# Separate pools for meta-token and rotary tiles, a later load of the key latents, and squares through PSUM in an encoder block

## The chip, the cores and the metric

One Trainium2 chip, one core. The time is device microseconds of one execution. Of its engines, TensorE (PE) multiplies into PSUM, VectorE (DVE), ScalarE (ACT) and GpSimd (POOL) work elementwise, and SyncE (SP) only issues transfers, one after another. PSUM has eight banks of 128 x 512 fp32.

## The reference

The kernel computes one layer on 1024 tokens with 16 learned meta tokens ahead of them (L = 1040), width 1024, in fp32:

```python
u = rmsnorm(h, norm_mix_w)
rq, rk, rv, rg, a_cq, a_ckv, a_kr, a_gret, a_gmla = split(u @ w_in)
y_ret = (silu(rg) * head_group_norm(bidir_retention(rope(rq), rope(rk) / 8, rv))) @ w_ret_out
c_q, c_kv = rmsnorm(a_cq, q_norm_w), rmsnorm(a_ckv, kv_norm_w)        # ranks 384 and 256
q_nope, q_rope = split_heads(c_q @ w_uq);  q_rope = rope(q_rope);  k_rope = rope(a_kr)
k_nope, v = c_kv @ w_uk, c_kv @ w_uv
y_mla = attention(q_nope, q_rope, k_nope, k_rope, v) @ w_mla_out      # 8 heads
h = h + (sigmoid(a_gret) * y_ret + sigmoid(a_gmla) * y_mla) @ w_o
u = rmsnorm(h, norm_ffn_w)
h = h + (silu(u @ w_ffn_gate) * (u @ w_ffn_up)) @ w_ffn_down          # 2816 wide
out = rmsnorm(h, norm_final_w)[16:]
```

## The kernel before

All large products run in split precision: an operand becomes a high part (a cast on ACT) and a low part (a subtraction on DVE, `split`, L153 and L154, and L209 and L210 for weights), and three matmuls of 128 x 512 give one product. Most products use seven block products instead of eight (`seven` and `seven_out`): four 512-wide weight blocks are loaded, POOL forms their sums (L191 to L193, L207), `prod` runs the matmuls of one block product (L217), and `seven_out` combines the banks on DVE (L233 to L242) and hands four result blocks to a `post` function. The order of instructions on each engine is chosen ahead of the run by a list scheduler with its own model of time, which goes by the order of the program where several instructions are ready; each engine and the queue of SyncE then run in that order. A tile is taken from a pool with a fixed number of buffers; its next user waits until all users of the buffer are done, a transfer's landing included.

The stages that the change touches:

1. **Last projections** (about 540 to 600 us). After the retention core, `project_key` (projects the last third of the query latent and the shared key) and `project_kv` (the key-value latent) run. Each also has a tail for the 16 meta tokens: matmuls of 48 rows (L222) gather them in one PSUM bank, `meta_sum` adds two parts (L431 on ACT, L432 on DVE), a transposition (L779, L802) turns them, `latent_part` and `shared_key` scale, square, split and store them (L724 to L734, L750 to L764), and `latent_norm` makes the factors `sq_c` and `skv_c` (L160, L741 to L744). All of these tiles, even the 16-column ones, come from the pool `cr`, which has six buffers of 128 x 512 and serves the results of all projections too. `rest_gates` (L813) also takes a buffer of `cr` and loads a saved partial result `e_d` into it. Between these, `z_split` loads 28 tiles `z_d` of retention results (L839), four buffers deep, and splits them (L275, L276).
2. **Retention output pairs** (about 598 to 691 us). `ret_out(0)`, a second, a `third` and `ret_out(3)`, each 84 matmuls. Their block products go through four PSUM banks (`pm`), and `pc` has the other four. Their `ret_post` loads a gate tile from `g_d` into `cr` (L856), multiplies (L857) and stores `r_d` (L858). Meanwhile six query latents `cq` and four key latents `ckv` (high and low parts, two each), 512 and 520 KB each, are loaded (L909), spread over the pairs by `tc.issue_after`, and `skv_b`, a row broadcast to all partitions (L915). Matmuls on `cq` make the rotary queries; `rotary` (L890 to L900), called by `third_post` four times, takes two table tiles per half and two tiles per call from `cr`, turns them and stores `qr`.
3. **Start of attention** (from about 679 us). `heads_k` multiplies `ckv` (`t<-ckh,kh`), DVE scales by `skv_b` into `kf` (L973); `heads_q` multiplies `cq`; the values `vt` need `ckv` too (`o<-vh,ckh`).
4. **Output projection** (`w_o`, about 1016 to 1108 us). For each token half `c` and block `m`: 24 matmuls, a residual addition on DVE (L1216), scaled blocks and, for `c` = 1, the block sums for the seven-product scheme (L1226 to L1240, one subtraction on POOL at L1236), then the square on ACT (L1245) and its addition to `ssum[c]` on POOL (L1246). `norm(c)` sums over partitions with eight matmuls of one column (L1197), takes root and reciprocal (L1201, L1202) and spreads the result with matmuls (L174) and a copy (L177).
5. **Feed-forward gate.** The first pair's first four block products are begun for three of the four input blocks, before the rest.

Of the kernel before, what the change touches and what calls it, by code (L numbers as in the profile page):

```python
# [17 lines left out]
P = 128  # L18
# [3 lines left out]
NM = 16  # L22
# [26 lines left out]
def build(nc, tc, A, out):  # L49
# [133 lines left out]
    def seven(pools, srcs, blocks, meta=None):  # L183
# [10 lines left out]
        side = {"11": a11, "t2": s2, "t3": a21, "n1": s1, "21": a12, "t4": a22, "22": s2}  # L194
        banks, w, begun = {}, {}, []

        def prod(b, qs=range(nq)):
            k = BANK[b]
            begins = k not in banks
            if begins:  # L200
# [51 lines left out]
    with ExitStack() as c1:  # L252
# [69 lines left out]
        with ExitStack() as c2:  # L322
# [89 lines left out]
            with tc.issue_after(made[0].ins), tc.issue_after(made[1].ins):  # L412
# [3 lines left out]
                for q in range(4):  # L416
                    U[q]["22"] = bsplit("22", x22[q])
            rest_out([(seven(w7, win(0), U), es[0], rg_post(0)),
                      (seven((wb, wf, wh1, wl1, pc), win(1), U), es[1], rg_post(1))], cr)
        mf = sb(mid, "factor", 1, side="right")  # L420
        rstd_b = mk(mf, (P, L), "rstd_b")
        lss = mk(mf, (P, L), "lss")
# [6 lines left out]
        def meta_sum(ps, lo, n):  # L429
            t = slot(cr)[:NM, :n]  # L430
            act.copy(t, ps[32:48, lo : lo + n])  # L431
            dve.tensor_add(t, ps[0:NM, lo : lo + n], t)  # L432
            return t
# [115 lines left out]
        def project_rope(j, key):  # L549
# [19 lines left out]
            if key:  # L569
                x = meta_sum(ps, 0, 256).rearrange("t (h c) -> t h c", c=64)  # L570
                y = slot(cr)[:NM, :256].rearrange("t (h c) -> t h c", c=64)

# [148 lines left out]
        def latent_part(t, c, dst, col, first):  # L721
            n = c.stop - c.start
            hi = slot(cr, F32R)[:, :n]
            act.mul(hi, t, col)  # L724
            if first:
                act.square(lss[:, c], t)
            else:
                q = slot(cr)[:, :n]
                act.square(q, t)
                dve.tensor_add(lss[:, c], lss[:, c], q)  # L730
            lo = slot(cr)[:, :n]
            dve.scalar_tensor_tensor(lo, t, col, f(hi), ALU.mult, ALU.subtract)
            store(dst[0][:, c], f(hi))
            store(dst[1][:, c], lo)  # L734
# [14 lines left out]
        def shared_key(ks, c):  # L749
            n = c.stop - c.start  # L750
            ca, sa = slot(cr)[:48, :n], slot(cr)[:48, :n]
            load(ca, A["cM"][:48, c])
            load(sa, A["sM"][:48, c])
            sb_, kh = slot(cr)[:48, :n], slot(cr, F32R)[:48, :n]
            dve.tensor_mul(ks, ks, rstd_b[:48, c])
# [34 lines left out]
        def project_key():  # L790
# [11 lines left out]
            pe.transpose(pt[:48, :NM], t, ident[:NM, :NM])  # L802
            ks = slot(cr)[:48, :NM]
            act.copy(ks, pt[:48, :NM])
# [60 lines left out]
        cq = [(mk(ap, (P, S), f"cqh{k}", F32R), mk(ap, (P, S), f"cql{k}", F32R)) for k in range(3)]  # L865
        ckv = [tuple(mk(ap, (P, 1152), f"ck{j}{k}", F32R)[:, :L] for j in "hl") for k in range(2)]
        swp = sb(right, "skv", 1, side="right")
        skv_b = mk(swp, (P, L), "skv_b")
        fill(swp, 112)
        wa = sb(right, "wa", 1, side="right")  # L870
        rot = ExitStack()
        wt = sb(rot, "rotary", 1, side="right")

        qr_d = [[mk(dram, (P, S), f"qr{i}{j}") for j in range(2)] for i in range(2)]
        wx, xx, tables = [], {}, []

        def wx_load(i):
            raw = slot(cr)[:, :384]
            load(raw, A["w_uq"][4 + i])
            hi = mk(wa, (P, 384), ("qh", "qr")[i], F32R)  # L880
            low = mk(wt, (P, 384), "xl", F32R) if i else mk(wa, (P, 384), "ql", F32R)
            act.copy(hi, raw)
            dve.tensor_sub(low, raw, f(hi))
            wx.append((hi, low))

        def rotary(lo, n, i):
            c = slice(lo, lo + n)
            if i == 0:
                tables[:] = slot(cr), slot(cr)
                load(tables[0], A["cM"][:, c])  # L890
                load(tables[1], A["sM"][:, c])
            ta, tb_ = slot(cr), slot(cr)
            dve.tensor_mul(ta, xx[lo, i], tables[0])
# [11 lines left out]
        wx_load(1)  # L905
        for i, (dst, src) in enumerate([(t, cq_d[k][j]) for k in range(3) for j, t in enumerate(cq[k])] + [
                (t, ckv_d[k][j]) for k in range(2) for j, t in enumerate(ckv[k])]):
            with tc.issue_after(issued[1 + i * 3 // 5].ins):
                load(f(dst), src)  # L909
# [4 lines left out]
        store(n_d, rowc)  # L914
        load(skv_b, n_d.rearrange("b i -> (b i)")[:L].unsqueeze(0).broadcast_to([P, L]))  # L915
        third = seven(w7, A["w_ro"][2], Z)
# [11 lines left out]
        seven_out(third, cr, third_post)  # L928
        rot.close()
        ret_out(3)  # L930

# [204 lines left out]
    with ExitStack() as c1:  # L1136
# [71 lines left out]
        for c in range(2):  # L1208
            for m in range(KT):
# [21 lines left out]
                else:  # L1231
# [3 lines left out]
                    t7["t2"] = split(t2, bt, bt)  # L1235
                    pool.tensor_sub(g12, g12, g22)  # L1236
                    t7["t3"] = split(g12, bt, bt)
# [3 lines left out]
                if m == 0:  # L1241
                    act.square(ssum[c], hm)
                else:
                    t = slot(xr)
                    act.square(t, hm)  # L1245
                    pool.tensor_add(ssum[c], ssum[c], t)  # L1246
            norm(c, slice(0, 512))

        w7 = (wr3, ws3, wh3, wl3, pm)
        for j in range(11):  # L1250
# [19 lines left out]
            if j == 0:  # L1270
                for b in NAMES[:4]:
                    prod(b, range(3))
                    rest[b] = range(3, 4)
            seven_out(prod, xr, gate_post, rest)
# [182 lines left out]
```

## Time and profile before

| | us |
|---|---|
| median of 3 timed runs | 1775.89 (1775.68 to 1776.03) |
| the profiled execution | 1780.81 |
| its span, first to last instruction | 1779.0 |
| TensorE busy in the span | 1714.6 |
| granted clock, mean over the span | 0.987 of full speed |

The time of a run is about that of the profiled span; the profiled execution was 4.9 us slower than the median of the timed runs. TensorE's busy time counts matmuls that overlap in a pipeline, so a stretch at full pace shows about 112 matmuls of 512 columns in 25 us.

### The profile page before, as it was taken

The numbers are of one execution on the slowest core, as the hardware profiler recorded it, in microseconds if no ns is written. First come the engines' busy times: TensorE is split into PE (matmuls) and PEld (weight loads), VectorE is DVE, ScalarE is ACT, GpSimd is POOL, SyncE is SP. The second block draws the span as 40 slices with busy tenths as digits, with TensorE's granted clock in tenths as the row PEclk, the third lists the DMA queues.
The fourth block names the chain that finished last, engine by engine and source line by source line (L and its number), as shares of the span: only waits on it lengthen the run. The fifth ranks groups of instructions, "written<-read, shape, count | busy, mean of one in ns | idle before, by whom it ended". The sixth has DMA issues, their size and how long they took to land.

```text
span 1779.0 us, 26433 instructions
## 1 busy us (share of the span) xinstructions
PE 1714.6 (96%) x8804; PEld 1443.9 (81%) x8804; DVE 1339.0 (75%) x2448; ACT 861.1 (48%) x1614; POOL 790.1 (44%) x605
## 2 busy tenths in 40 slices
PE   8999999999999899999999999899999999999997
PEld 6788777788887677899998888788888888787787
DVE  7845778788888857888888758767666666987965
ACT  7425766344324523788787346433332232543434
POOL 1322257674554321234332524666676566533422
PEclk9999999999999899999999999999999999999999
DMA  7733823566546785111112754233323333854512
GB/s 255 240 101 119 295 85 117 180 201 213 189 158 230 213 301 179 28 34 40 30 59 69 231 187 162 66 101 119 101 95 101 107 105 101 286 176 123 154 57 95
DMA packets 145433, 253.59 MB, mean 143 GB/s; under 512 B 18889, under 2 KB 36738, under 8 KB 145298
## 3 DMA queue, kind: packets, MB, share of 16 engines
q1 hardware_dynamic: 145298, 251.92, 43.5%
q8 instruction: 69, 1.13, 0.3%
q14 instruction: 66, 0.54, 0.1%
HBM read 174.93 MB, written 76.85 MB: 142 GB/s over the span
## 4 chain that ended last, share of the span: by engine, by line
PE 49%; DVE 7%; DMA 3%; ACT 3%; issue 2%; SPq 0%; POOL 0%; DVEq 0%; ACTq 0%; POOLq 0%
PE mm L217 29%; PE o L1041 3%; PE mm L138 3%; PE mm L137 3%; PE mm L139 3%; PE t L1012 2%; DVE slot L154 2%; PE s L137 1%; PE s L138 1%; PE s L139 1%; DMA slot<-g_d 1%; DMA slot<-f_d 1%; DVE slot L210 1%; DVE ptl L1015 1%; PE o L137 1%
## 5 line engine op out<-in xcount | busy, mean ns | idle before, releaser
L217 PE MATMUL mm<-slot,slot 128*128 128x512 f32 x2604 | 598.3, 392 | 8.4 <-ACT slot L209 3.7
L217 PEld LDWEIGHTS mm<-slot,slot 128*128 128x128 f32 x2604 | 490.6, 189 | 115.0 <-DVE slot L210 5.5
L209 ACT CAST slot<-slot 128x512 fp32r<-128x512 f32 (+1 forms) x413 | 246.1, 598 | 465.9 <-PE mm L217 395.0
L210 DVE TENSOR_TENSOR slot<-slot,slot 128x512 fp32r<-128x512 f32 (+1 forms) x413 | 361.6, 877 | 71.5 <-ACT slot L209 70.4
L217 PE MATMUL mm<-ht,slot 128*128 128x512 f32 x648 | 219.6, 400 | 7.4 <-DVE slot L210 3.4
L217 PE MATMUL mm<-h,slot 128*128 128x512 f32 x536 | 184.4, 403 | 0.0
L191 POOL TENSOR_TENSOR slot<-slot,slot 128x512 f32<-128x512 f32 (+1 forms) x61 | 85.3, 1398 | 220.0 <-DMA slot<-in_w_u 50.7
L207 POOL TENSOR_TENSOR slot<-slot,slot 128x512 f32<-128x512 f32 (+1 forms) x61 | 84.7, 1390 | 185.1 <-DVE slot L210 173.1
L217 PEld LDWEIGHTS mm<-ht,slot 128*128 128x128 f32 x648 | 122.1, 190 | 35.1 <-DVE slot L210 5.6
L154 DVE TENSOR_TENSOR slot<-slot,slot 128x512 fp32r<-128x512 f32 x137 | 117.5, 872 | 20.6 <-ACT slot L153 20.0
L217 PE MATMUL mm<-lt,slot 128*128 128x512 f32 x324 | 128.7, 397 | 0.0
L153 ACT CAST slot<-slot 128x512 fp32r<-128x512 f32 x137 | 83.3, 619 | 76.9 <-DMA slot<-f_d 30.3
L192 POOL TENSOR_TENSOR slot<-slot,slot 128x512 f32<-128x512 f32 (+1 forms) x61 | 86.0, 1410 | 77.6 <-DVE slot L210 65.6
L217 PEld LDWEIGHTS mm<-h,slot 128*128 128x128 f32 x536 | 101.2, 190 | 21.6 <-DVE slot L210 0.6
L1002 DVE TENSOR_SCALAR_CACHE_REDUCE pr<-s,sq_c 128x384 f32<-128x384 f32 (+1 forms) x192 | 103.3, 573 | 7.9 <-PE t L1020 3.8
L217 PE MATMUL mm<-l,slot 128*128 128x512 f32 x268 | 106.6, 398 | 0.0
L139 PE MATMUL mm<-slot,slot 128*128 128x512 f32 (+1 forms) x288 | 105.3, 366 | 0.0
L138 PE MATMUL mm<-slot,slot 128*128 128x512 f32 (+1 forms) x288 | 105.3, 366 | 0.0
L137 PE MATMUL mm<-slot,slot 128*128 128x512 f32 (+1 forms) x288 | 105.1, 367 | 0.0
L1015 DVE TENSOR_TENSOR ptl<-t,pth 128x512 fp32r<-128x512 f32 x128 | 85.7, 685 | 18.2 <-ACT pth L1014 17.6
L1046 POOL TENSOR_TENSOR oa<-oa,ob 64x256 f32<-64x256 f32 x32 | 24.0, 751 | 154.5 <-ACT ob L1045 149.1
L193 POOL TENSOR_TENSOR slot<-slot,slot 128x512 f32<-128x512 f32 (+1 forms) x61 | 88.2, 1445 | 1.4
(365 smaller groups left out, 3506.0 us busy)
## 6 DMA issues: line engine op xcount, KB each, us to landing
slot<-in_w_in SPq DMA_DIRECT2D x106, 256.0 KB
f_d<-slot SPq DMA_DIRECT2D x71, 256.0 KB
slot<-f_d SPq DMA_DIRECT2D x71, 256.0 KB
slot<-in_xT SPq DMA_DIRECT2D x48, 256.0 KB
slot<-z_d SPq DMA_DIRECT2D x44, 256.0 KB
slot<-in_w_g SPq DMA_DIRECT2D x44, 256.0 KB
slot<-in_w_u SPq DMA_DIRECT2D x44, 256.0 KB
slot<-in_w_dq SPq DMA_DIRECT2D x48, 192.0 KB
```

What stands on the lines that cost most here:

```text
L137: pe.matmul(ps, sh, mh, start=start, stop=False)
L138: pe.matmul(ps, sh, ml, start=False, stop=False)
L139: pe.matmul(ps, sl, mh, start=False, stop=stop)
L154: dve.tensor_sub(lo, t, f(hi))
L191: pool.tensor_add(s1, a21, a22)
L192: pool.tensor_sub(s2, s1, a11)
L193: pool.tensor_sub(a21, a21, a11)
L209: act.copy(hi, side[b])
L210: dve.tensor_sub(low, side[b], f(hi))
L217: pe.matmul(ps, sw[:, ks], sx, start=begins and q == qs[0] and i == 0, stop=q == nq - 1 and i == 2, skip_group_check=True)
L1002: dve.tensor_scalar(pr[:, c], ps[:, :n], sq_c[:, qb : qb + 1], None, ALU.mult, ALU.max, accum_out=mx[:, j : j + 1])
L1015: dve.tensor_sub(pt[1][d], tp, f(pt[0])[d])
```

## The change

- **Pools.** Two new pools beside the other `mid` tiles: `small` (eight 16-column buffers) and `sums` (two 256-column buffers). `meta_sum`, the rotary sum of the keys' meta tokens, and the tails of `latent_part` and `shared_key` take their tiles there and not in `cr`.
- **Rotary.** A pool `rotary_r` of eleven 512-column buffers holds the raw rotary weights, the tables and the tiles of `rotary`; `cr` is left to the output pairs.
- **Key latents.** `ckv` and `skv_b` are no longer allocated ahead of the pairs; they take the place of the rotary pools once these are closed, after `third`, and are loaded in the program's order just before `ret_out(3)`. The six `cq` loads are tied to the pairs at nearly the same points as before.
- **Output projection.** Squares go to a PSUM bank of the pool `pm` (seven banks), and DVE adds them to `ssum`; the subtraction at L1236 moves from POOL to DVE. `norm(0)` stands after both halves, `norm(1)` behind the first 36 matmuls of the gate. `prod` remembers which parts are done, so that the second call does the rest.

```diff
+        banks, w, begun, done = {}, {}, [], set()
         def prod(b, qs=range(nq)):
             k = BANK[b]
+            qs = [q for q in qs if (b, q) not in done]
+            done.update((b, q) for q in qs)
...
+        small, sums = sb(mid, "small", 8, side="right"), sb(mid, "sums", 2, side="right")
+        def work(n):
+            return slot(cr) if n > NM else mk(small, (P, NM), "small")
         def meta_sum(ps, lo, n):
-            t = slot(cr)[:NM, :n]
+            t = mk(sums, (P, 256), "sums")[:NM, :n]
...
         def latent_part(t, c, dst, col, first):
-            hi = slot(cr, F32R)[:, :n]
+            hi = work(n).bitcast(F32R)[:, :n]
...
         def shared_key(ks, c):
-            ca, sa = slot(cr)[:48, :n], slot(cr)[:48, :n]
+            ca, sa = work(n)[:48, :n], work(n)[:48, :n]
...
-        ckv = [tuple(mk(ap, (P, 1152), f"ck{j}{k}", F32R)[:, :L] for j in "hl") for k in range(2)]
-        swp = sb(right, "skv", 1, side="right")
-        skv_b = mk(swp, (P, L), "skv_b")
-        fill(swp, 112)
         wt = sb(rot, "rotary", 1, side="right")
+        rr_ = sb(rot, "rotary_r", 11, side="right")
...
-                tables[:] = slot(cr), slot(cr)
+                tables[:] = slot(rr_), slot(rr_)
-            ta, tb_ = slot(cr), slot(cr)
+            ta, tb_ = slot(rr_), slot(rr_)
...
-        for i, (dst, src) in enumerate([(t, cq_d[k][j]) for k in range(3) for j, t in enumerate(cq[k])] + [
-                (t, ckv_d[k][j]) for k in range(2) for j, t in enumerate(ckv[k])]):
-            with tc.issue_after(issued[1 + i * 3 // 5].ins):
+        for i, (dst, src) in enumerate([(t, cq_d[k][j]) for k in range(3) for j, t in enumerate(cq[k])]):
+            with tc.issue_after(issued[1 + i // 2].ins):
                 load(f(dst), src)
...
-        load(skv_b, n_d.rearrange("b i -> (b i)")[:L].unsqueeze(0).broadcast_to([P, L]))
...
         seven_out(third, cr, third_post)
         rot.close()
+        ap = sb(right, "latent_kv", 1, side="right")
+        ckv = [tuple(mk(ap, (P, 1152), f"ck{j}{k}", F32R)[:, :L] for j in "hl") for k in range(2)]
+        swp = sb(right, "skv", 1, side="right")
+        skv_b = mk(swp, (P, L), "skv_b")
+        load(skv_b, n_d.rearrange("b i -> (b i)")[:L].unsqueeze(0).broadcast_to([P, L]))
+        for k in range(2):
+            for j, t in enumerate(ckv[k]):
+                load(f(t), ckv_d[k][j])
         ret_out(3)
...
-                    pool.tensor_sub(g12, g12, g22)
+                    dve.tensor_sub(g12, g12, g22)
...
-                    t = slot(xr)
+                    t = mk(pm, (P, 512), "mm")
                     act.square(t, hm)
-                    pool.tensor_add(ssum[c], ssum[c], t)
-            norm(c, slice(0, 512))
+                    dve.tensor_add(ssum[c], t, ssum[c])
+        norm(0, slice(0, 512))
...
             if j == 0:
                 for b in NAMES[:4]:
                     prod(b, range(3))
-                    rest[b] = range(3, 4)
+                norm(1, slice(0, 512))
```

## Rows read from the trace of the kernel before

**Rows 1.** The profile page of the whole execution: busy us of each engine, share of the span, count of instructions.

```profile
PE 1714.6 (96%) x8804; PEld 1443.9 (81%) x8804; DVE 1339.0 (75%) x2448; ACT 861.1 (48%) x1614; POOL 790.1 (44%) x605
```

**Rows 2.** A table by stage: stretch of the span, its length, busy us of each engine with its count of instructions, granted clock, mean share of the DMA engines, GB/s. 540:612 holds the last projections and the splitting of the retention results, 675:705 the end of the retention output pairs and the start of attention, 1071:1123 the second half of the output projection.

```profile
540.00:612.00 72.00, 61.40 (x292) 49.65 (x292) 60.78 (x97) 38.32 (x73) 29.29 (x19) 0.88 0.72 232
675.00:705.00 30.00, 26.00 (x116) 22.42 (x115) 21.42 (x34) 10.27 (x20) 6.87 (x9) 0.89 0.57 180
...
1071.00:1123.00 52.00, 47.39 (x216) 38.81 (x214) 43.37 (x51) 29.12 (x50) 25.47 (x16) 1.00 0.42 137
```

**Rows 3.** The same columns for five short stretches in which the granted clock is about one half (the lower of its two levels, 1.2 GHz instead of 2.4).

```profile
556.90:563.90 7.00, 7.00 (x48) 6.79 (x48) 4.37 (x15) 2.12 (x5) 4.04 (x4) 0.51 0.41 135
584.20:587.80 3.60, 3.60 (x10) 2.35 (x8) 2.84 (x4) 1.86 (x4) 0.61 (x1) 0.53 0.80 217
591.10:598.00 6.90, 3.83 (x11) 3.05 (x10) 5.57 (x15) 3.92 (x8) 0.73 (x1) 0.51 0.70 199
693.50:700.40 6.90, 6.02 (x17) 5.38 (x18) 5.96 (x10) 2.53 (x6) 3.15 (x3) 0.51 0.54 160
1123.60:1130.40 6.80, 6.80 (x20) 5.57 (x20) 6.80 (x10) 3.01 (x7) 3.00 (x2) 0.50 0.14 44
```

**Rows 4.** Instructions of TensorE in order of time, the four of 550 to 600 us ahead of which it stood idle longest: start, us, engine, line, operation, and in brackets the idle time before and its releaser.

```profile
556.20 0.19 PE L802 MATMUL mm<-ident,slot 16*48 16x16 f32 x1 [1.48 <-DVE slot L432]
...
581.31 0.23 PE L779 MATMUL mm<-ident,slot 16*128 16x16 f32 x1 [1.57 <-DVE slot L432]
...
590.93 0.20 PE L160 MATMUL mm<-ones,lss 128*16 128x1 f32 x2 [2.89 <-DVE lss L730]
594.21 0.76 PE L217 MATMUL mm<-ht,slot 128*128 128x512 f32 x1 [3.07 <-DVE skv_c L744]
```

**Rows 5.** Instructions of ScalarE, VectorE and the queue of SyncE in the same stretch, in the same form.

```profile
553.84 0.19 ACT L431 COPY slot<-mm 16x48 f32<-16x48 f32 x1 [0.88 <-DVE slot L732]
...
593.37 0.69 DVE L302 TENSOR_TENSOR slot<-mm,slot 128x512 f32<-128x512 f32 x1 [0.27 <-DMA slot<-e_d]
...
590.07 0.32 SPq L733 DMA_DIRECT2D ckv_d<-slot  x1
590.43 0.42 SPq L813 DMA_DIRECT2D slot<-e_d  x1
```

**Rows 6.** The end of the retention output pairs and the start of attention, from the timelines of TensorE, VectorE and the queue of SyncE, in the same form.

```profile
694.38 0.66 PE L137 MATMUL t<-cqh,qh 128*128 128x384 f32 x1 [3.27 <-DVE kf L973]
...
692.49 0.69 DVE L857 TENSOR_TENSOR slot<-slot,slot 128x512 f32<-128x512 f32 x1 [3.49 <-DMA slot<-g_d]
693.10 1.13 DVE L973 TENSOR_TENSOR kf<-t,skv_b 64x384 f32<-64x384 f32 x2
...
669.06 0.68 DVE L242 TENSOR_TENSOR slot<-slot,mm 128x512 f32<-128x512 f32 x1
...
685.13 0.32 SPq L900 DMA_DIRECT2D qr<-slot  x1
...
688.05 0.94 SPq L856 DMA_DIRECT2D slot<-g_d  x2
```

**Rows 7.** Sizes of transfers issued from 600 to 700 us (line form: transfer, queue, kind, count, KB each), and the groups of TensorE instructions from 675 to 725 us that read the latents (name, shape, count, busy us, mean ns).

```profile
ckh<-ckv_d SPq DMA_DIRECT2D x2, 520.0 KB
...
L137 PE MATMUL o<-vh,ckh 128*128 128x512 f32 (+1 forms) x18 | 7.9, 440 | 0.0
...
L137 PE MATMUL t<-cqh,qh 128*128 128x384 f32 (+1 forms) x9 | 3.6, 396 | 3.3 <-DVE kf L973 3.3
...
L137 PE MATMUL t<-ckh,kh 128*128 128x384 f32 (+1 forms) x6 | 2.0, 340 | 0.7 <-DVE slot L894 0.7
```

**Rows 8.** Groups of instructions of 1071 to 1125 us, by line and shape: count, busy us, mean ns of one, idle time of the engine before them and its releasers.

```profile
L154 DVE TENSOR_TENSOR slot<-slot,slot 128x512 fp32r<-128x512 f32 x19 | 17.1, 918 | 5.3 <-ACT slot L153 5.2
...
L1246 POOL TENSOR_TENSOR ssum<-ssum,slot 128x512 f32<-128x512 f32 x7 | 11.2, 1594 | 10.6 <-ACT slot L1245 10.6
...
L1236 POOL TENSOR_TENSOR slot<-slot,slot 128x512 f32<-128x512 f32 x4 | 6.5, 1633 | 13.0 <-ACT slot L1233 13.0
...
L1216 DVE TENSOR_TENSOR slot<-mm,slot 128x512 f32<-128x512 f32 x7 | 4.8, 684 | 1.5 <-PE mm L139 1.1 <-DMA slot<-in_xT 0.4
```

**Rows 9.** The seam between the output projection and the feed-forward gate, from the timelines of VectorE, GpSimd, ScalarE and TensorE, in the form of rows 4.

```profile
1112.76 1.76 DVE L154 TENSOR_TENSOR slot<-slot,slot 128x512 fp32r<-128x512 f32 x1
...
1115.64 0.68 DVE L1216 TENSOR_TENSOR slot<-mm,slot 128x512 f32<-128x512 f32 x1
...
1118.71 1.62 POOL L191 TENSOR_TENSOR slot<-slot,slot 128x512 f32<-128x512 f32 x1 [4.74 <-DMA slot<-in_w_u]
1120.29 1.71 POOL L1236 TENSOR_TENSOR slot<-slot,slot 128x512 f32<-128x512 f32 x1
1121.96 1.26 POOL L1246 TENSOR_TENSOR ssum<-ssum,slot 128x512 f32<-128x512 f32 x1
...
1108.39 4.70 PE L217 MATMUL mm<-slot,slot 128*128 128x512 f32 x20
1115.17 5.30 PE L217 MATMUL mm<-slot,slot 128*128 128x512 f32 x22 [2.08 <-DVE slot L210]
1123.28 1.59 PE L1197 MATMUL r<-ones,ssum 128*128 128x1 f32 x8 [2.80 <-POOL ssum L1246]
1124.73 7.01 PE L217 MATMUL mm<-slot,slot 128*128 128x512 f32 x18
```

More of the change, by code (lines that the diff above doesn't have):

```diff
@@ L194, in seven @@
         side = {"11": a11, "t2": s2, "t3": a21, "n1": s1, "21": a12, "t4": a22, "22": s2}
-        banks, w, begun = {}, {}, []
+        banks, w, begun, done = {}, {}, [], set()
         def prod(b, qs=range(nq)):
             k = BANK[b]
+            qs = [q for q in qs if (b, q) not in done]
+            done.update((b, q) for q in qs)
             begins = k not in banks
@@ L570, in project_rope @@
                 x = meta_sum(ps, 0, 256).rearrange("t (h c) -> t h c", c=64)
-                y = slot(cr)[:NM, :256].rearrange("t (h c) -> t h c", c=64)
+                y = mk(sums, (P, 256), "sums")[:NM].rearrange("t (h c) -> t h c", c=64)
                 def table(i, lo, n):
@@ L727, in latent_part @@
             else:
-                q = slot(cr)[:, :n]
+                q = work(n)[:, :n]
                 act.square(q, t)
                 dve.tensor_add(lss[:, c], lss[:, c], q)
-            lo = slot(cr)[:, :n]
+            lo = work(n)[:, :n]
             dve.scalar_tensor_tensor(lo, t, col, f(hi), ALU.mult, ALU.subtract)
@@ L750, in shared_key @@
             n = c.stop - c.start
-            ca, sa = slot(cr)[:48, :n], slot(cr)[:48, :n]
+            ca, sa = work(n)[:48, :n], work(n)[:48, :n]
             load(ca, A["cM"][:48, c])
             load(sa, A["sM"][:48, c])
-            sb_, kh = slot(cr)[:48, :n], slot(cr, F32R)[:48, :n]
+            sb_, kh = work(n)[:48, :n], work(n).bitcast(F32R)[:48, :n]
             dve.tensor_mul(ks, ks, rstd_b[:48, c])
@@ L802, in project_key @@
             pe.transpose(pt[:48, :NM], t, ident[:NM, :NM])
-            ks = slot(cr)[:48, :NM]
+            ks = work(NM)[:48, :NM]
             act.copy(ks, pt[:48, :NM])
@@ L877, in wx_load @@
         def wx_load(i):
-            raw = slot(cr)[:, :384]
+            raw = slot(rr_)[:, :384]
             load(raw, A["w_uq"][4 + i])
```

## Prediction

> **What bounds the kernel now.** I read the page first, then a table by stage, the waits of TensorE, and the timelines around its longest waits. The page shows TensorE busy for 96% of the span and no other engine near that [rows 1]: the kernel runs at the pace of its matmuls, and a change of the other engines counts only where TensorE stands idle or at its lower clock. The table by stage shows where that is: 61.4 of 72 us busy at a granted clock of 0.88 around the last projections, 26.0 of 30 us at 0.89 where the output pairs give way to attention, 47.4 of 52 us ahead of the feed-forward gate [rows 2]. The five stretches at the lower level, 1.2 GHz, lie in the same places [rows 3], each behind or among waits or one-column and thin matmuls. At that level a matmul takes twice its time, so a stretch costs half of TensorE's busy time in it; as a check, 18 matmuls took 7.01 us behind the seam and 20 took 4.70 ahead of it [rows 9]. The full pace is then (4.70 - 0.39) / 19 = 0.227 us for 512 columns, 0.39 being the time of a single one.
>
> The change touches just these three places. I cost them as A, B and C.
>
> **A, small tiles out of the shared pool.** Four waits of TensorE are 1.48, 1.57, 2.89 and 3.07 us, 9.0 in all, and each ends with a step of the meta tokens' tails or of `rest_gates` [rows 4]. The first two wait for `meta_sum`. Ahead of its copy (L431) ScalarE had waited until a 512-column instruction on another tile, L732, was over [rows 5]: that is a buffer of `cr` coming free. With `sums` this sum can be made as soon as its matmuls are done, microseconds earlier, and TensorE's transposition behind it does not wait: I take off both, 3.05. The third ends a chain of transposition, scaling, square and sum which stays, at some 1.3 us by the sizes of its parts; the delays between its parts go. I take off 1.5. The fourth, put down to `skv_c`, is really the load of `e_d`: VectorE's L302 started at 593.37, released by that load, and frees the bank that TensorE needs. The load was issued at 590.43, straight behind the store of a tail (L733 at 590.07) in the queue of SyncE [rows 5]. With earlier tails it goes earlier; I take off 2.5. Stalls: 7.0.
>
> The lower clock in this stage costs 7.0 / 2 + 3.6 / 2 + 3.83 / 2 = 7.2 us [rows 3]. The first stretch lies on the one-column sums and the 48-row matmuls, which the change leaves, so I credit 1 us in all. A limit from above: VectorE is busy 60.78 of the 72 us [rows 2], so no more than 11.2 us can go here, and what TensorE would wait for next is the splitting of the `z_d` tiles on VectorE, four raw buffers at a time. A = -8, between 0 (the order of the queues stays as it is) and -11.
>
> **B, rotary pool and later key latents.** TensorE waits 3.27 us at 694.38 for `kf`. `kf` stands behind an L857 on VectorE that waited 3.49 us for a `g_d` load, issued only from 688.05 on [rows 6]. Without rotary tiles in `cr` this load finds a buffer sooner. The stretch at the lower clock behind it costs 6.02 / 2 = 3.0 [rows 3]. So 6.3 us can be had.
>
> Against that stand the five late loads, four of 520 KB [rows 7] and `skv_b`, 1040 columns on 128 partitions and so as large: 2.66 MB. Around 675 to 705 us the transfer engines are 0.57 busy at 180 GB/s [rows 2], 316 GB/s at full share: 8.4 us if the loads have the engines alone, 2.66 MB / 136 GB/s = 19.6 us if all present traffic keeps its pace. They can start when the last rotary store has landed. That store is issued at 685.13 now, but held up by `cr`; the last combination of `third` is at 669.06 [rows 6], and two rotary calls of four VectorE steps and one ScalarE step, all near 0.69 us, one behind the other, end near 676. A store takes some 3 us to land, as the `e_d` load did (590.43 to 593.37 [rows 5]), and the loads run from 679 to between 687 and 699. TensorE wants them when `ret_out(3)` is over. It is over at 690.8 now, with 18 `heads_k` matmuls inside it (six on each of three lines [rows 7]; by width 12 x 0.170 + 6 x 0.121 = 2.8 us) that must now come behind it: at 688. The 27 `heads_q` matmuls (nine on each line, 4.1 us) need no key latents and can go first: 692. So the new wait is between 0 and 11 us. The output pair's own loads and stores are nearly through by then, so I take a landing near 690, a wait of 2 and 1.3 for the clock: 3.3. B = -3, between -6.3 and +8 (11 of wait and 3.4 of clock).
>
> **C, squares through PSUM.** The gate's matmuls begin at 1108.39, those of the output projection being through, yet VectorE reads their last bank at 1115.64: it is 7 us behind. Then come two ScalarE steps, and POOL, which first waits 4.74 us for a weight load and runs L191, then L1236 and L1246 until 1123.2; TensorE has waited 2.80 us for that sum, after 2.08 for a weight split [rows 9]. The lower clock then costs 6.8 / 2 = 3.4 [rows 3]: 8.3 us together. With subtraction and addition on VectorE, the last square's sum is ready about four 0.7 us steps behind 1115.64, near 1119, before the 42 gate matmuls are over at 1120.5; the 2.80 goes, and with it most of the clock's cost.
>
> VectorE pays 7 additions and 4 subtractions in this half: 11 x 0.684 = 7.5 us (an addition that reads PSUM takes 0.684, L1216 [rows 8]); the 7 additions of the first half have room. It gains back what POOL cost it: two-operand instructions on SBUF take 0.68 alone and 1.76 beside POOL [rows 9], 0.918 in the mean [rows 8]. With about 40 of them in 51 [rows 2], 40 x 0.234 = 9.4 us for 16 POOL instructions, 0.59 each, times 11 = 6.4. VectorE so loses 1.1 us of a 52 us stage in which it was idle for 8.6. I take 7 of the 8.3: C = -7, between -8.3 and +5 (VectorE gives nothing back and the seam waits 7.5 us longer, less the 2.80).
>
> The Trainium skill (SBUF — State Buffer, section "Who interferes with whom") says that a VectorE instruction with two SBUF inputs and a GpSimd instruction that reads SBUF exclude each other for the whole instruction, while one with a single SBUF input is free of it; by that up to 11 x 1.6 = 17 us would come back and C would be -8.3, the total -19.3. The trace agrees as to who is stretched, but its mean is a third of that price, and I go by the mean.
>
> The Trainium skill (Perfetto Trace Analysis, section "Optimizing Scalar/DVE Operations") speaks against the change: an access to PSUM costs VectorE about 125 ns where SBUF costs about 60; by that the 14 additions are 0.9 us dearer, an estimate, and the total -17. Here L1216 from PSUM takes 0.684 and an undisturbed SBUF one 0.68, so I add nothing.
>
> Moving `norm(0)` costs nothing: the same 8 + 8 small matmuls, covered at either place by gate or output matmuls; uncovered they are the 1.59 + 1.05 us that the second norm shows.
>
> **The sum.** -8 - 3 - 7 = -18 against 1780.81: 1762.8. That execution is 4.9 us over the timed median, so in timed runs 1775.89 - 18 = 1758.
>
> **Rivals.**
> *The latents come late.* As the upper end of B: -8 + 8 - 7 = -7, 1769. For it: all present traffic stays; against: `heads_q` as cover.
> *The splits set the pace.* TensorE, early, waits for the `z_d` splits instead: A = -1, total -11, 1765. For it: VectorE at 84% there; against: it has idle gaps of its own.
> *Nothing is gained.* A list scheduler orders all engines anew, and a wait that closes opens at a neighbour: -1, 1775. Against: the waits have causes that the change removes.
> *Slower: SyncE's queue is held.* The five loads precede `ret_out(3)` in the program. If the scheduler puts them in the queue near 672 and the last rotary store lands only at its present 688, all behind them (`g_d` loads, `r_d` stores, weights) stands for 16 us and then shares 8.4 us with them; TensorE has four banks for these products and stops. With 3.4 for the clock this is 27.8 us, less the 6.3: B = +21.5, total +6.5, 1782. It decides from a loss of about 25 us gross on, which takes off A, C and the 6.3. For it: SyncE issues in order, and L857 shows what a late `g_d` load does. Against: rotary should end ten microseconds sooner.
>
> **Chances.** Forecast 0.55 (own range 1749 to 1767), late latents 0.13, splits 0.09, nothing gained 0.09, queue held 0.14. 0.2% (3.6 us) is about what a measurement tells from no change. Faster: 0.54 + 0.12 + 0.08 + 0.02 = 0.76; same: 0.01 + 0.01 + 0.01 + 0.07 = 0.10; slower: 0.14. The range 1747 to 1778 leaves out the held queue and a little of the best end (A, B and C at their bounds: -25.6, 1750; with all of A's clock, some more).
>
> **What would show it.** A: the waits at L802, L779 and L160 gone, L813 issued earlier, a shorter stage before `ret_out(0)`. B: no wait of L857 for `g_d` near the pair's end; the loads of `ckh` landing before TensorE's first `t<-ckh`. C: no POOL in the sum, L1197 without a wait, no stretch at 1.2 GHz behind it. The prediction is wrong if TensorE waits over 5 us for `ckh`, or if waits of the same size appear where none were.

## The result, and the profile after

The changed kernel takes 1763.38 us (median of 6 runs, 1762.36 to 1770.21); the kernel before, beside it, 1776.4 (6 runs, 1775.68 to 1779.39). The ratio is 0.9933, 95% interval 0.9915 to 0.995: some 12 us faster. The forecast was 1758, its own range 1749 to 1767.

The page's line of busy times, as in [rows 1]:

```profile
PE 1707.4 (97%) x8804; PEld 1436.7 (82%) x8804; DVE 1343.5 (76%) x2466; ACT 859.6 (49%) x1615; POOL 761.7 (43%) x586
```

TensorE does the same 8804 matmuls; GpSimd has 19 instructions less. The three stages of [rows 2], in the same columns:

```profile
540.00:612.00 72.00, 63.50 (x286) 48.83 (x286) 64.61 (x97) 40.15 (x75) 29.66 (x19) 0.93 0.74 244
675.00:705.00 30.00, 27.88 (x136) 23.97 (x135) 21.00 (x42) 14.29 (x26) 7.15 (x9) 0.94 0.43 131
1071.00:1123.00 52.00, 50.28 (x228) 41.05 (x228) 46.82 (x65) 29.67 (x52) 16.73 (x12) 1.00 0.39 124
```

And the stretches of 540 to 705 us, and the one of 1123.6, that answer to [rows 3]:

```profile
556.20:563.20 7.00, 7.00 (x25) 5.40 (x26) 5.73 (x12) 2.29 (x6) 1.28 (x1) 0.51 0.50 172
583.50:587.00 3.50, 3.15 (x7) 2.48 (x8) 3.50 (x8) 1.24 (x2) 1.10 (x1) 0.51 0.84 268
685.90:689.40 3.50, 3.50 (x10) 2.75 (x9) 3.14 (x6) 2.15 (x5) 2.12 (x2) 0.51 0.84 241
...
1123.60:1130.40 6.80, 6.80 (x31) 5.63 (x30) 4.48 (x5) 3.39 (x6) 6.49 (x6) 1.00 0.12 41
```

The stretch at 591.1 is gone, the one at 693.5 is half as long and comes at 686, the one behind the seam at 1123.6 runs at full clock. The one at 557 is as it was: that belongs to A. In an execution of the same program on another chip none comes near 686 and the one at 584 lasts 6.8 us, not 3.4: these lengths also vary from one execution to the next.

**A.** TensorE, 543 to 585 us, the answers to [rows 4]:

```profile
544.51 0.19 PE L810 MATMUL mm<-ident,sums 16*48 16x16 f32 x1 [0.65 <-DVE sums L440]
...
555.82 1.46 PE L160 MATMUL mm<-ones,lss 128*128 128x1 f32 x8 [3.42 <-DVE lss L738]
...
579.27 1.05 PE L160 MATMUL mm<-ones,lss 128*128 128x1 f32 x8 [0.28 <-DVE lss L738]
580.36 0.23 PE L787 MATMUL mm<-ident,sums 16*128 16x16 f32 x1
581.94 0.50 PE L219 MATMUL mm<-h,slot 128*128 128x512 f32 x1 [1.35 <-ACT slot L211]
583.85 1.22 PE L219 MATMUL mm<-h,slot 128*128 128x512 f32 x2 [1.18 <-DVE slot L212]
...
590.53 0.20 PE L160 MATMUL mm<-ones,lss 128*16 128x1 f32 x2
```

The four waits of before (1.48, 1.57, 2.89, 3.07) are 0.65 and then nothing: the transposition L787, the token sum over the 16 meta columns at 590.53 and the matmuls behind it start without one. But another token sum (L160, the query latents') now waits 3.42, where before it started right behind the transposition L802, a third one 0.28, and matmuls wait 1.35 and 1.18 for weight splits. VectorE and GpSimd ahead of the first of these sums:

```profile
550.32 1.25 DVE L764 TENSOR_TENSOR small<-small,small 48x16 f32<-48x16 f32 x1 [1.88 <-DMA small<-in_cM]
551.60 1.20 DVE L765 TENSOR_TENSOR small<-small,small 16x16 f32<-16x16 f32 x1
552.83 1.19 DVE L766 TENSOR_TENSOR small<-small,small 16x16 f32<-16x16 f32 x1
554.05 1.71 DVE L738 TENSOR_TENSOR lss<-lss,slot 128x512 f32<-128x512 f32 x1
```

```profile
550.25 1.29 POOL L712 TENSOR_TENSOR slot<-slot,slot 128x512 f32<-128x512 f32 x1
551.50 1.28 POOL L191 TENSOR_TENSOR slot<-slot,slot 128x512 f32<-128x512 f32 x1
552.73 1.26 POOL L713 TENSOR_TENSOR slot<-slot,slot 128x512 f32<-128x512 f32 x1
553.95 1.26 POOL L193 TENSOR_TENSOR slot<-slot,slot 128x512 f32<-128x512 f32 x1
```

The tail, earlier now, is a wait for its own table (1.88) and then three instructions on 16 columns of 1.2 us each, one beside each GpSimd instruction; in the trace of before the two on 16 partitions (L757, L758, at 559.8) took 0.16 and 0.17. All of it stands ahead of L738, for which TensorE waits.

**B.** SyncE's queue, against [rows 6]:

```profile
614.30 0.84 SPq L884 DMA_DIRECT2D slot<-in_w_uq  x2
...
654.24 0.32 SPq L905 DMA_DIRECT2D qr<-slot  x1
654.66 0.38 SPq L937 DMA_DIRECT2D skv_b<-n_d  x1
655.09 0.47 SPq L940 DMA_DIRECT2D ckh<-ckv_d  x1
...
659.70 0.53 SPq L940 DMA_DIRECT2D ckl<-ckv_d  x1
```

and TensorE:

```profile
621.58 0.39 PE L137 MATMUL mm<-cqh,qh 128*128 128x512 f32 x1
...
671.92 0.33 PE L137 MATMUL t<-ckh,kh 128*128 128x384 f32 x1
...
685.52 0.50 PE L137 MATMUL o<-vh,ckh 128*128 128x512 f32 x1 [1.77 <-DVE slot L244]
...
689.97 0.34 PE L137 MATMUL t<-cqh,qh 128*128 128x384 f32 x1
```

and what that last wait stands behind, on SyncE's queue and VectorE:

```profile
680.08 0.91 SPq L864 DMA_DIRECT2D slot<-g_d  x2
...
684.18 0.69 DVE L865 TENSOR_TENSOR slot<-slot,slot 128x512 f32<-128x512 f32 x1 [3.94 <-issue]
```

The last rotary store is issued at 654.24 (before: 685.13), the late loads straight behind it, at 654.66 to 659.70. The first `t<-ckh` is 12 us after the last of them was issued and does not wait. The wait of 3.27 for `kf` is gone; 1.77 for a combination of the output pair (L244) is there. L244 follows L865 on VectorE (the L857 of before), which waits 3.94 for its `g_d` tile; before, it waited 3.49. The profile names no releaser for that wait, but L865 starts as the first of the loads issued at 680.08 has landed (at 684.10).

**C.** TensorE at the seam, against [rows 9]:

```profile
1106.45 0.95 PE L1208 MATMUL r<-ones,ssum 128*128 128x1 f32 x8
1107.26 3.18 PE L219 MATMUL mm<-slot,slot 128*128 128x512 f32 x12
1112.15 1.05 PE L174 MATMUL r<-ident,r2c 128*128 128x128 f32 x7 [1.72 <-DVE r2c L1213]
```

The 2.80 for `ssum` and the 2.08 for a weight split are gone; 1.72 for the norm's spread is new.

### The profile page after: what moved, and what is told of

Same layout as the page of the kernel before. It is cut to its first block, busy times and chain, and to the rows that moved or that the text cites. A ratio compares the mean times of both kernels' runs of the same rounds, so it can differ in the third digit from the quotient of the medians.

```text
span 1761.2 us, 26371 instructions
## 1 busy us (share of the span) xinstructions
PE 1707.4 (97%) x8804; PEld 1436.7 (82%) x8804; DVE 1343.5 (76%) x2466; ACT 859.6 (49%) x1615; POOL 761.7 (43%) x586
## 4 chain that ended last, share of the span: by engine, by line
PE 49%; DVE 6%; ACT 2%; DMA 2%; issue 2%; SPq 0%; DVEq 0%; ACTq 0%
PE mm L219 28%; PE o L1052 3%; PE mm L138 3%; PE mm L139 3%; PE mm L137 3%; PE t L1023 2%; DVE slot L154 2%; PE s L137 1%; PE s L139 1%; PE s L138 1%; DMA slot<-f_d 1%; DMA slot<-in_xT 1%; PE o L137 1%; PE o L139 1%; PE o L138 1%
## 5 line engine op out<-in xcount | busy, mean ns | idle before, releaser
L191 POOL TENSOR_TENSOR slot<-slot,slot 128x512 f32<-128x512 f32 (+1 forms) x61 | 84.5, 1385 | 300.4 <-DMA slot<-in_w_g 81.0
L154 DVE TENSOR_TENSOR slot<-slot,slot 128x512 fp32r<-128x512 f32 x137 | 112.6, 837 | 13.2 <-ACT slot L153 12.3
L192 POOL TENSOR_TENSOR slot<-slot,slot 128x512 f32<-128x512 f32 (+1 forms) x61 | 85.8, 1406 | 81.7 <-DVE slot L212 60.7
L1026 DVE TENSOR_TENSOR ptl<-t,pth 128x512 fp32r<-128x512 f32 x128 | 85.8, 685 | 17.8 <-ACT pth L1025 17.2
```

Of the source, the lines that this page charges most:

```text
L154: dve.tensor_sub(lo, t, f(hi))
L192: pool.tensor_sub(s2, s1, a11)
L1026: dve.tensor_sub(pt[1][d], tp, f(pt[0])[d])
```

## Experiments

Every timed comparison is with the kernel before on the same chip. Beside it stands what one profiled execution shows: how much time TensorE loses (+) or gains (-) against before over a stretch of before's time, compared where it has done the same number of matmul columns. Each half-clock stretch that comes or goes between executions moves such a number by 1.7 us for 3.4 us of length. How far chance moves it can be read where nothing was changed: the four kernels with parts of C alone show +0.6 to -2.6 in the first column, those with parts of A and B alone +0.3 to -1.5 in the second.

```
kernel                       ratio   95% interval       540-740   1080-1140  (us)
after                        0.9933  0.9915 to 0.9950    -7.3      -5.8
after, second chip           0.9929  0.9912 to 0.9945    -8.7      -5.9
A alone                      0.9998  0.9989 to 1.0007    -0.7      +0.3
B alone                      0.9995  0.9983 to 1.0006    -1.4      -1.5
A and B                      0.9950  0.9932 to 0.9968    -8.1      -1.4
A, late loads only           1.0026  1.0015 to 1.0037    +4.2      -0.9
C alone                      0.9966  0.9953 to 0.9979    +0.6      -5.5
C, norms in place            0.9951  0.9935 to 0.9966    -2.6      -6.3
C, squares in SBUF           0.9974  0.9961 to 0.9987    -0.9      -3.0
C, norms' places only        0.9985  0.9974 to 0.9996    -1.7       0.0
after, norm ahead of tail    0.9912  0.9898 to 0.9925    -9.9      -5.3
after, tail from PSUM        0.9923  0.9908 to 0.9938   -10.4      -5.4
after, tail behind the sum   0.9908  0.9890 to 0.9926   -10.5      -4.0
```

### Which part brings what

A alone (only the pools `small` and `sums`), on the kernel before:

```
+        def work(n):
+            return slot(cr) if n > NM else mk(small, (P, NM), "small")
...
+            t = mk(sums, (P, 256), "sums")[:NM, :n]
```

> The kernel before with part A alone (pools for the meta tokens' tiles and sums). Theory of the study: A is worth -2.5 us (range -1 to -4), because the two waits for the meta sums go while a new wait for the sum of squares of the latents' tail (3.6 us, TensorE's transposition after VectorE's addition on 16 columns) and the half-clock stretch behind it stay: the tail's tiny VectorE instructions take 1.2 us each, beside GpSimd. The prediction's A was -8. Rival: A is worth its -8 and the other parts lose it again; then this run is near 1768. Rival: the order written anew moves everything, and A alone is within 1 us of the kernel before.

B alone (only the hunks with `rr_` and `latent_kv`):

```
+        rr_ = sb(rot, "rotary_r", 11, side="right")
...
+            raw = slot(rr_)[:, :384]
...
+                load(f(t), ckv_d[k][j])
         ret_out(3)
```

> The kernel before with part B alone (rotary pool, late key latents and late skv_b). Theory of the study: -4 us (range -2 to -6): the wait of 3.3 us for kf near the end of the output pairs and the wait ahead of the first o<-pt go, a short half-clock stretch is left; the late loads are no wait, since the rotary products come 20 us earlier than in the kernel before and the t<-ckh matmuls start after 670. Prediction: -3. Rival: the latents come late by themselves when A is not there (the meta tail's work is later), a wait of several us for ckh and about +3.

C alone (only the hunks with `done`, `ssum` and `norm`):

```
+                    t = mk(pm, (P, 512), "mm")
+                    dve.tensor_add(ssum[c], t, ssum[c])
+        norm(0, slice(0, 512))
```

> The kernel before with part C alone (squares through PSUM, subtraction and additions on VectorE, norms moved). Theory of the study: -6 us (range -4 to -7): the wait of 2.8 us for the last sum and the half-clock stretch behind it (3.4) go; a wait of 1.9 us for the spread of the first norm is new at the moved place. Prediction: -7. Rival: the gain is the start's (the first 60 us differ by 3.5 us between the two profiled executions with the same TensorE order), then C alone is worth -3 and A, B and C together less than 13.

Measured: C as expected, -6 us. A and B alone are within 1 us of the kernel before (intervals -2.0 to +1.2 and -3.0 to +1.1 us): A's -2.5 and B's -4 did not come, and of A's rivals the last has the number. The trace of A alone shows where its gain goes. TensorE, and the load and the cast of the weights that it waits for:

```profile
644.73 0.50 PE L137 MATMUL mm<-cqh,qh 128*128 128x512 f32 x1 [2.13 <-ACT qh L888]
...
691.33 0.41 PE L137 MATMUL t<-cqh,qh 128*128 128x384 f32 x1 [3.48 <-DVE kf L979]
```

```profile
637.39 0.33 SPq L885 DMA_DIRECT2D slot<-in_w_uq  x1
...
644.16 0.52 ACT L888 CAST qh<-slot 128x384 fp32r<-128x384 f32 x1
```

At 620 us A alone is 2.1 us ahead of where it stood against before at 540, and it stops again at the rotary products: their weights are loaded through `cr`, from 637.39 on, where the kernel after loads them at 614, and the cast comes 6.8 us after the load was issued. In B alone A's stage is as before, and TensorE then stops 1.84 us at 656.14 for a weight split on VectorE, with a half-clock stretch behind it.

A and B together (the hunks of both):

> Parts A and B together, without C. A alone and B alone came out as the kernel before (ratios 0.9998 and 0.9995), C alone at -6, all three at about -12. Theory of the study: A and B need each other: A brings TensorE 4 us early to 620 us, where A alone gives it back at the rotary products (a wait of 2.3 us for the weights' split qh, which is loaded through the pool cr, at 642 us, and a half-clock stretch behind it) and at kf (3.65 us); with the rotary pool both waits go. So A and B together are worth what is missing: -6 (range -4 to -8). Rival: the missing part is a difference of chips or of runs; then A and B together are within 2 us of the kernel before.

Measured: 0.995, about -9 us (interval -12 to -6, expected -4 to -8), and neither of A's two stops is in its trace. The parts are not a sum: 0 and 0 alone, -9 together.

A, and of B the late loads alone; the rotary tiles stay in `cr`:

```
-        ckv = [tuple(mk(ap, (P, 1152), f"ck{j}{k}", F32R)[:, :L] for j in "hl") for k in range(2)]
 ...
         rot.close()
+        ckv = [tuple(mk(ap, (P, 1152), f"ck{j}{k}", F32R)[:, :L] for j in "hl") for k in range(2)]
+        load(skv_b, n_d.rearrange("b i -> (b i)")[:L].unsqueeze(0).broadcast_to([P, L]))
...
         ret_out(3)
```

> Part A and of part B only the late loads of the key latents and of skv_b: the rotary tiles stay in the pool cr. Theory of the study: what makes A's gain last is that rotary tiles do not take buffers of cr, so that without the rotary pool the waits for qh at 642 and for kf at 690 stay: within 2 us of the kernel before. Rival: it is the 2.66 MB of loads taken out of a stretch where the transfer engines are 0.85 busy that lets the weights come in time: then -5 or more, as with the whole of A and B.

Measured: 1.0026, 4.6 us slower than before; neither the theory nor the rival had that. The cast of the rotary weights, TensorE, and the chain of waits ahead of TensorE's longest one:

```profile
638.68 0.51 ACT L884 CAST qh<-slot 128x384 fp32r<-128x384 f32 x1 [5.30 <-DMA slot<-in_w_uq]
```

```profile
680.33 0.69 PE L137 MATMUL t<-ckh,kh 128*128 128x384 f32 x1 [7.13 <-DVE slot L896]
```

```profile
669.16 4.46 DMA vr<-in_w_uv
673.65 1.05 ACT vh L132
674.72 0.89 DVE vl L133
...
675.87 0.68 DVE slot L896
...
679.68 0.61 DVE slot L896
```

The rival's first step is there: with the key latents' loads out of this stretch the weights, still loaded through `cr` (issued at 635.29), are cast 3.4 us later instead of 6.8, and TensorE does not stop at the rotary products. At 640 us this kernel is 2.5 us ahead of where it stood against before at 540. It loses that and more at 680: the third `t<-ckh,kh` waits 7.13 us, not for its latents (issued at 649.0 to 651.9) but for a rotary step (L896) on VectorE, and the rotary steps stand behind a split of `vr` whose load is late. So the late loads by themselves take away A's first stop, and rotary steps that are still under way when the heads begin undo it. The rotary pool with the key latents at their old place was not run; what it gives by itself stays open.

The kernel after once more, on that chip:

> The kernel after once more, beside the others on one chip. Both theories: -12 to -13 against the kernel before. It bounds what the order of the meta tail (latents' norm first) gave: that kernel came to 0.9912 of the kernel before; if this one comes to 0.993 again, the swap is worth -3, if to 0.991, nothing.

Measured: 0.9929, as expected.

### Inside C

The additions and the subtraction on VectorE, squares in PSUM, norms where they were (the hunks with `done` and `norm` left out):

> Of part C only the engines: squares through PSUM, the additions and the subtraction on VectorE; the norms stay where they were. Theory of the study: the sum of squares is ready in time once GpSimd is out of it, so the wait of 3.0 us for ssum and the half-clock stretch behind it go, and nearly all of C comes: -5 (range -4 to -7). Rival: the gain is the norms' place (gate products are put ahead of the second norm and cover the wait); then the wait at the norm stays and this is within 2 us of the kernel before.

Only the norms' places (the other hunks left out):

> Of part C only the norms' new places: additions and subtraction stay on GpSimd, squares in SBUF. Theory of the study: the norm's sum comes no earlier and TensorE has 42 gate matmuls fewer ahead of it or as many: within 2 us of the kernel before, with a wait for ssum of 2 to 3 us. Rival: the order of the gate products and norms is the cause of C's gain: -4 or more.

Squares in SBUF:

```
-                    t = mk(pm, (P, 512), "mm")
+                    t = slot(xr)
```

> Part C alone, but with the squares in the SBUF pool xr as before, additions and subtraction on VectorE, norms moved. Theory of the study: what counts is that GpSimd is out of the chain of sums, so the wait for ssum and the half-clock stretch go as in C alone: -6 (range -3 to -8), and the additions, now with two SBUF inputs, are up to 1 us longer where GpSimd runs beside them. Rival: the squares' way through PSUM counts, because xr's buffers hold the chain up; then most of the wait of 3.0 us for ssum stays, -2 or less.

Measured: with the norms in place all of C is there (0.9951, some -9 us where -4 to -7 was expected; -6.3 in the stage). The norms' places alone do nothing in the stage and bring 2.7 us in the timed runs (0.9985, interval -4.6 to -0.7), yet they do take away the wait for `ssum`, against the expectation; what stays is a stop for a weight split on VectorE and the lower clock:

```profile
1108.65 0.73 PE L219 MATMUL mm<-slot,slot 128*128 128x512 f32 x2 [2.25 <-DVE slot L212]
1110.54 2.07 PE L174 MATMUL r<-ident,r2c 128*128 128x128 f32 x8 [1.15 <-DVE r2c L1204]
...
1119.40 0.95 PE L1199 MATMUL r<-ones,ssum 128*128 128x1 f32 x8
```

So it is the work taken off GpSimd that carries C; whether the additions or the subtraction count more was not separated. With the squares in SBUF the timed gain (-4.6) is within the expected range and its interval overlaps that of C alone; in the stage it is -3.0 instead of -5.5, with a stop of 1.41 at the norm that the trace puts down to ScalarE's L177 and not to the sum, and, against the expectation, a half-clock stretch of 3.4 us from 1120.9 on. What the way through PSUM is worth by itself stays open, at 0 to 2.5 us.

### The wait that A brought

Three versions of the kernel after. First the norm placed ahead of the tail in the program:

```
             act.copy(ks, pt[:48, :NM])
+            latent_norm(sq_c, 3, 96.0**-0.5, range(NB))
             shared_key(ks, tail)
-            latent_norm(sq_c, 3, 96.0**-0.5, range(NB))
```

> The kernel after, with the latents' norm on the query latents placed ahead of the shared key of the meta tail in the program. Theory of the study: the wait of 3.6 us of the transposition behind the tail's sum of squares goes if the tail's VectorE steps on 16 columns stand behind the sum in VectorE's order, with the half-clock stretch behind it (3.4 us): -4 against the kernel after, about 1759. Rival: the tail's own sum is what is late, not what stands ahead of it; then it is as the kernel after, 1763.

In its trace the tail's steps still stand ahead of the sum on VectorE, and the wait is 3.81 instead of 3.42: the change of place did reorder other instructions (TensorE has a new wait of 3.45 at 583.13), but not these. Its timed ratio, 0.9912, is so no test of that wait. Then the tail's shared key read from PSUM:

```
-            ks = work(NM)[:48, :NM]
-            act.copy(ks, pt[:48, :NM])
-            shared_key(ks, tail)
+            shared_key(pt[:48, :NM], tail)
```

> The kernel after, with the meta tail's shared key read from PSUM, where its transposition put it, without the copy to SBUF; nothing else. L764 to L766 (48x16 and 16x16) then have one SBUF input and one PSUM input. Theory of the study: these took 1.25, 1.20 and 1.19 us because two-SBUF-input instructions on VectorE and GpSimd's exclude each other in turn; from PSUM they take about 0.16 each, the sum L738 is 3 us earlier and the wait near 552 us falls from 3.6 to about 1: -2 to -3 against the kernel after. Rival: any VectorE instruction with an SBUF input is stretched beside GpSimd; then they still take about 1.2 us each and nothing changes.

VectorE of that kernel:

```profile
549.31 0.17 DVE L766 TENSOR_TENSOR small<-mm,small 16x16 f32<-16x16 f32 x1
549.50 1.72 DVE L770 TENSOR_TENSOR slot<-slot,slot 48x512 f32<-48x512 f32 x1
551.15 1.25 DVE L767 TENSOR_TENSOR small<-small,small 16x16 f32<-16x16 f32 x1
...
555.32 1.75 DVE L738 TENSOR_TENSOR lss<-lss,slot 128x512 f32<-128x512 f32 x1
```

L764 to L766 take 0.16 to 0.17 each, but they were over when GpSimd's run of five began (549.39), so this does not show that PSUM frees them; the next five with two SBUF inputs were stretched in their place, and the wait is 3.30. Last, the tail's steps held behind the last addition on VectorE by an ordering edge:

```
+            latent_norm(sq_c, 3, 96.0**-0.5, range(NB))
+            with tc.issue_after(sums_q[0].ins), tc.issue_after(sums_q[1].ins):
+                shared_key(ks, tail)
```

> The kernel after, with the meta tail's shared-key steps on VectorE queued behind the last addition to the sums of squares (the earlier try, which only moved the norm in the program, left them ahead of it on VectorE). Theory of the study: the wait of 3.6 us at the norm's token sums near 552 us falls to under 1 us, and with it some of the half-clock stretch behind it: -3 against the kernel after (range -1 to -6), about 0.991 of the kernel before. Rival: what TensorE would wait for next is the splitting of the z_d tiles or GpSimd's sums of them, so that the wait reappears within 30 us: as the kernel after, 0.993.

TensorE of this kernel:

```profile
555.88 1.00 PE L160 MATMUL mm<-ones,lss 128*128 128x1 f32 x8
561.39 0.47 PE L219 MATMUL mm<-ht,slot 128*128 128x512 f32 x1 [0.96 <-DVE small L771]
...
573.11 0.50 PE L219 MATMUL mm<-hn,slot 128*128 128x512 f32 x1 [2.54 <-ACT slot L211]
```

The wait at L160 is gone, and 17 us later there is one of 2.54 for a weight split: from 540 to 620 TensorE is idle 9.0 us where it is idle 8.8 in the kernel after, and gains 2.5 us where that gains 2.2. In this stage the rival was right that the wait comes back within 30 us, though not for the `z_d` tiles that it named. The timed ratio, 0.9908, is the theory's 0.991 and not the rival's 0.993. The ratios of all three, 0.9908 to 0.9923, are lower than after's 0.9929 and 0.9933, but the intervals overlap and they come from different chips: that one of them beats the kernel after is not shown, nor is the contrary.

## Why the prediction was right, and where it was off

The sum was -18; timed it is -12 to -13. The two profiled executions are 17.8 us apart, but that agreement is chance: 3.5 us of it arise in the first 60 us, where TensorE's order is the same in both, and unchanged beginnings in ten of the twelve profiled experiments are 2 to 3.5 us faster than that of before's too. The profiled execution of before began slowly.

**A, forecast -8 (bounds 0 to -11): -2.2 in its stage, and 0 by itself.** Right: of the waits at L802, L779, L160 and behind `e_d` only 0.65 is left, and the `e_d` load is issued at 576.05 instead of 590.43. Wrong is the step "stalls: 7.0", which took the waits off and put nothing in their place: over the same 320 matmuls, from 540 to 620 us of before, TensorE is idle 8.8 us instead of 11.4, 2.6 less. The prediction's own sign of being wrong, waits of the same size where none were, is there with the 3.42. The matmuls' own time did not fall: the stretch with 3.83 us of work at the lower clock went, where 1 us was credited for the clock, but the 207 matmuls of 512 columns at full clock took 0.245 us from start to start instead of 0.238, 1.6 us in all; why stays open. The rival "the splits set the pace" with A = -1 comes nearer to the size of this stage, and its 1765 nearer to 1763.4 than 1758 does. But it named the splits of the `z_d` tiles, and TensorE waits for weight splits (1.35, 1.18 and 0.98, the longest) and for the tail's steps behind GpSimd, which hold more of it.

**B, forecast -3 (bounds -6.3 to +8): it makes A's gain last.** The two together were forecast at -11 and give -7.3 to -9. The failed step is the schedule of the rotary calls: "near 676" came from moving the end of the chain only. With buffers of its own the weights' load goes at 614.3 instead of 641.5, the products begin at 621.6 instead of 649.2, and the last store is 31 us earlier. So the late loads, expected from 679 on with a wait of 2 and 1.3 of clock, were never in question, and both rivals on them (1769 and 1782) fell with that. Half of the 6.3 us came: the wait for `kf` went, 1.77 and half of the stretch stayed. The step "this load finds a buffer sooner" failed as well: the `g_d` load goes at 680.08 instead of 688.05, about as far ahead as TensorE itself is by then (7.5 us), and VectorE waits 3.94 for it instead of 3.49. What stands behind that wait is now L244 and not `kf`, so the sign "no wait of L857 for `g_d`" did not come. What the sum also missed is that these parts depend on each other; adding A and B assumed that a gain at 600 us reaches the end, while with A alone a load at 637 us through the same pool, among the key latents' loads, took it back.

**C, forecast -7 (bounds -8.3 to +5): -5.8 in its stage, -6 timed by itself.** Right in mechanism: no GpSimd in the sum, no wait for it, no stretch at 1.2 GHz behind it. Mis-sized by the norm's spread: the move "costs nothing" left a wait of 1.72 that the trace of before does not have. Mis-sized too is what VectorE gets back: between 1071 and 1130 us, 14 of its 128x512 instructions with two SBUF inputs were stretched, by 11.3 us in all, and 9 by 7.4 after: 3.9 where 6.4 was credited.

With -7.3 and -5.8 and a half-clock stretch at 880.5 in this execution (+1.5) the parts give -11.6, near the 12 that was timed. That the total fell into the forecast's range owes something to luck: A's stage fell 5.8 short of its -8, and from 620 to 740 us, where B lies, 5.1 came where 3 was forecast.

## What to carry to other kernels

A wait that ends on a shared pool's buffer is rarely alone: ask what the earlier instruction will stand in front of in its own engine's order, and price the next wait before taking off the first. When two parts of a change lie one behind the other on the same pool or queue, the first one's gain counts only if the second keeps it; test them together and apart. And one profiled execution against another can differ by several us in places that were not changed: compare at equal work, stage by stage.

## What the runs showed of the hardware

In these rows the stretching of VectorE by GpSimd goes by instructions and not by size: a 16x16 instruction (L765) took 1.20 us instead of 0.16, near the 1.28 of the GpSimd instruction beside it, and the 128x512 one (L738) 1.71 instead of 0.68, about 1.0 us more for either. The Trainium skill (SBUF — State Buffer, section "Who interferes with whom") states that a VectorE instruction with two SBUF inputs contends with one of GpSimd that reads SBUF, and that one with at most one SBUF input, outside the modes that use two ports, does not. The trace after agrees: between 1071 and 1130 us four of VectorE's two-operand additions, subtractions and products of 512 columns read PSUM and began under a GpSimd instruction: 0.69 us each, and 0.68 for the fifteen that began beside none; with both inputs in SBUF the nine that began so took 1.50 in the mean, the other 33 0.68. Two rows 1.5 us apart:

```profile
1088.75 0.69 DVE L1227 TENSOR_TENSOR slot<-mm,slot 128x512 f32<-128x512 f32 x1 [0.62 <-DMA slot<-in_xT]
...
1090.23 1.51 DVE L1245 TENSOR_TENSOR slot<-slot,slot 128x512 f32<-128x512 f32 x1 [0.19 <-ACT slot L1244]
```

GpSimd ran L191 under the first (from 1087.94, 1.33 us) and L192 under the second (from 1089.36, 1.83 us). The prediction's mean price (0.234 a piece) hid this: what matters is which instruction stands beside GpSimd's.
